# One-core streaming-encoder block: the output projection's mixes transposed one tile ahead, the up projection's products interleaved across groups

## The chip, the cores and the metric

The kernel runs on one core of a Trainium2 chip. The metric is the device time of one execution in microseconds; it was run three times, and one more execution was taken with the hardware profiler. The engines are called PE (matrix products), DVE (vector), ACT (scalar, activation functions), POOL (GpSimd) and SP, whose queue issues all transfers between HBM and the core's memory SBUF. PE writes its results to PSUM, of which the kernel uses eight banks of 512 fp32 columns by 128 rows.

## The reference

One layer of an encoder, all in fp32, over 1024 frames and 16 meta tokens in front of them. Cut to what matters here:

```
n = rms_norm(h); z = n @ w_in
u = silu(layer_norm(causal_conv(a * sigmoid(gate))))          # branch A, 512 columns
o = block_causal_attention(...)                               # branch B, 512 columns
mix = concat(rms_norm(u, conv_out_g), rms_norm(o, attn_out_g))
h = h + mix @ w_out                                           # output projection, 1024 x 1024
n2 = rms_norm(h, ffn_norm_g)
up = causal_depthwise_conv(n2 @ w_ffn_up, ffn_conv_w, ffn_conv_b)   # 1024 -> 2 x 2816, conv of 3 taps
g, val = up[..., :D_FF], up[..., D_FF:]
h = h + (silu(g) * val) @ w_ffn_down                          # 2816 -> 1024
out = rms_norm(h, final_norm_g)                               # meta tokens dropped
```

## The kernel before

Every fp32 product is made of reduced-precision ones. A value is split into a high part (a copy in the type fp32r, made by ACT, L167 for operands and L244 for down weights) and a low part (the difference, made by DVE, L168, or for down weights by POOL, L247), and each product takes three matmuls: high by high, high by low, low by high (`mm3`, L162 to L164). The program is written as one sequence; a scheduler then sets the order of each engine's instructions from the dependences and its own estimate of durations. So an engine's order isn't simply that of the code, but it follows it loosely.

**Output projection.** Tokens come in tiles of 128 rows, in the order 8, 0, 1, ..., 7; tile 8 holds the two meta rows that the later convolution needs. For tile t and branch g (0 is A, 1 is B) `mix_part` transposes the mix by four PE transposes into a bank `mt`, and splits it into `mx`. `project` multiplies it with the split weights: two banks `po`, 12 matmuls of 128x512 each. `add_branch` adds the scaled result to the residual `ht` on DVE (L967). In the loop over tiles, each step transposes the A mix of the tile two steps on, multiplies it at once, transposes the B mix of the tile two steps on, and multiplies the B mix of this tile.

**Norm and spread.** One step behind, `ffn_norm` takes the sum of squares (ACT L978), an inverse root by some ten small DVE instructions (L182 to L193) and the normed tile `n` (DVE L980; also called n2). `spread` transposes `n` into two banks `nt` and makes from it the operands of the up projection. These are kept for a scheme of the Strassen-Winograd kind: seven products in place of eight, on operands B11, B21 (tiles 8, 0 to 3) and B22, T1 to T4 (from tiles 4 to 7, `spread_second`: sums on DVE L861, L862 and POOL L864, L865, then splits). Each has a high and a low part, xB11h, xB11l and so on.

**Up projection.** 22 pairs of column blocks; pair i has 128 gate columns and 128 value columns. `up_weights` makes from two loaded blocks (`raw`) the seven weights A11, S3, S1, S2, A12, A22, S4, with four DVE sums (L888, L891, L894, L901) and seven splits into `uw`. The tokens form two column groups, c = 0 (258 wide) and c = 1 (256 wide). `up_pair` makes the seven products of one pair and group, each 12 matmuls (L920), in four banks `up`: A11·B11, S3·T3, S1·T1, S2·T2, A12·B21, A22·T4, S4·B22. S2·T2 is added in PSUM on top of A11·B11, A22·T4 on top of S3·T3, and S4·B22 on top of S1·T1. Between them ACT copies p1 and u2 out of PSUM (L925, L929), DVE makes u3 (`tmp`, L930) and the four quarters of the two rows (L931, L933, L935, L937). A22·T4 overwrites the bank that u3 is read from, so it can't start before u3 is made. Then `conv3` (ACT L1117, DVE L1118, L1119) for gate and value, the silu (ACT L1149), the product of the two (DVE L1151) and a store to `gated_d`. The weights of pair i+1 are made piece by piece while group c = 1 of pair i is written.

**Down projection.** For each half of the tokens and each of the 22 blocks k: the gated block is loaded from `gated_d` and split (`gate_split`, ACT L1163, DVE L1164), the weight block is split, and 24 matmuls of 128x512 add into eight banks `pd`. After it the final norm is applied and the result stored.

## Time and profile before

| | us |
|---|---|
| runs, lowest, median, highest | 1333.83, 1334.62, 1339.85 |
| the profiled execution | 1330.62 |
| its span, first to last instruction | 1328.8 |
| PE busy | 1211.3 (91%) |
| DVE busy | 901.9 (68%) |
| ACT busy | 544.3 (41%) |
| POOL busy | 332.9 (25%) |

The span of the profiled execution falls into the work ahead of the output projection (to about 455 us), the output projection with norm and spread (to 613), the up projection (to 1068) and the down projection with the final norm. Busy time of PE says only that matmuls were in it, not at which clock; the granted clock of a stretch is given beside it, 1.00 for the higher of its two levels (2.4 GHz) and 0.50 for the lower (1.2 GHz). An idle time in brackets stands ahead of an instruction and names who ended it; a name there is that of the last event seen, and can be a neighbour of the true one.

### The profile page before, as it was taken

How to read it: one execution, taken by the hardware profiler on the slowest of the kernel's cores; microseconds unless marked ns; L12 is line 12 of the kernel's file. 1: busy time of each engine (PE TensorE's matmuls, PEld its weight loads, DVE VectorE, ACT ScalarE, POOL GpSimd, SP SyncE). 2: the span in 40 equal slices, each digit the busy share in tenths (PEclk: the TensorE clock that was granted, in tenths of full speed). 3: DMA queues.
4: the chain of work that ended last, by engine and by line, in shares of the span. 5: the costliest groups of instructions: out<-in, count | busy, mean ns of one | idle time of the engine just before them, and what ended most of it. 6: DMA issues, size and time to landing. Idle time of an engine off the chain costs nothing.

```text
span 1328.8 us, 20317 instructions
## 1 busy us (share of the span) xinstructions
PE 1211.3 (91%) x7867; PEld 1112.6 (84%) x7867; DVE 901.9 (68%) x1600; ACT 544.3 (41%) x1049; POOL 332.9 (25%) x309
## 2 busy tenths in 40 slices
PE   6899598979989888868999999999999979999997
PEld 6799598969877767657999999999999968888886
DVE  6799979848888755487778787787877731233134
ACT  7212344356765622233434443344433343323322
POOL 3244655124556400020000000000000045514540
PEclk9899889989998899897999999999999989999999
DMA  7110110883432121132121212212122245725521
GB/s 254 52 37 13 36 48 31 205 225 92 108 101 80 33 80 64 48 111 96 49 95 65 80 64 80 95 66 80 64 80 94 78 148 194 241 102 183 188 106 64
DMA packets 47397, 130.54 MB, mean 98 GB/s; under 512 B 8282, under 2 KB 12954, under 8 KB 47300
## 3 DMA queue, kind: packets, MB, share of 16 engines
q1 hardware_dynamic: 47300, 129.24, 30.1%
q8 instruction: 62, 1.02, 0.3%
q14 instruction: 35, 0.29, 0.1%
HBM read 98.36 MB, written 28.33 MB: 95 GB/s over the span
## 4 chain that ended last, share of the span: by engine, by line
PE 41%; DVE 12%; ACT 2%; issue 1%; DVEq 0%; ACTq 0%
PE up L920 22%; PE pd L162 6%; PE pd L163 6%; PE pd L164 6%; DVE tg L1118 4%; DVE tg L1119 4%; ACT tg L1117 2%; DVE tg L1151 2%; DVE row L937 1%; DVE tmp L930 1%; DVE t L188 0%; DVE n L980 0%; DVE xT2l L168 0%; PE nt L157 0%; DVE ta L862 0%
## 5 line engine op out<-in xcount | busy, mean ns | idle before, releaser
L247 POOL TENSOR_TENSOR wl<-raw,wh 128x1024 fp32r<-128x1024 f32 (+3 forms) x75 | 196.1, 2620 | 668.6 <-ACT wh L244 645.9
L162 PE MATMUL pd<-wh,gp 128*128 128x512 f32 (+1 forms) x356 | 139.0, 396 | 8.1 <-ACT wh L244 8.1
L163 PE MATMUL pd<-wl,gp 128*128 128x512 f32 (+1 forms) x356 | 139.3, 391 | 0.0
L164 PE MATMUL pd<-wh,gp 128*128 128x512 f32 (+1 forms) x356 | 139.1, 391 | 0.0
L1164 DVE TENSOR_TENSOR gp<-gt,gp 128x512 fp32r<-128x512 f32 x44 | 42.1, 961 | 129.2 <-ACT gp L1163 129.2
L1117 ACT ACTIVATE tg<-row,ffnw 128x1024 f32<-128x1024 f32 x44 | 52.3, 1237 | 126.2 <-DVE row L937 126.2
L681 POOL TENSOR_TENSOR pl<-p,ph 128x320 fp32r<-128x320 f32 (+11 forms) x76 | 79.6, 1052 | 79.5 <-ACT ph L679 48.7
L162 PEld LDWEIGHTS pd<-wh,gp 128*128 128x128 f32 x356 | 68.0, 191 | 23.2 <-ACT wh L244 8.3
L920 PE MATMUL up<-xT4h,uw 128*128 128x258 f32 (+1 forms) x352 | 72.1, 288 | 12.5 <-DVE tmp L930 12.5
L163 PEld LDWEIGHTS pd<-wl,gp 128*128 128x128 f32 x356 | 67.2, 189 | 14.9 <-POOL wl L247 0.2
L164 PEld LDWEIGHTS pd<-wh,gp 128*128 128x128 f32 x356 | 67.2, 189 | 14.9
L920 PE MATMUL up<-xB11h,uw 128*128 128x258 f32 (+1 forms) x352 | 73.3, 286 | 3.9 <-ACT uw L167 2.4
L1118 DVE SCALAR_TENSOR_TENSOR tg<-row,ffnw,tg 128x1024 f32<-128x1024 f32 x44 | 54.6, 1282 | 28.9 <-ACT tg L1117 28.9
L920 PE MATMUL up<-xT3h,uw 128*128 128x258 f32 (+1 forms) x352 | 72.4, 286 | 0.5 <-ACT uw L167 0.5
L920 PE MATMUL up<-xB21h,uw 128*128 128x258 f32 (+1 forms) x352 | 72.5, 281 | 0.0
L673 ACT ACTIVATE p<-st 128x320 f32<-128x320 f32 (+11 forms) x120 | 53.4, 454 | 44.7 <-PE st L671 17.0
L920 PEld LDWEIGHTS up<-xT4h,uw 128*128 128x128 f32 x352 | 57.2, 189 | 16.8 <-DVE tmp L930 16.8
L920 PE MATMUL up<-xT1h,uw 128*128 128x258 f32 (+1 forms) x352 | 70.9, 282 | 0.0
L920 PE MATMUL up<-xB22h,uw 128*128 128x258 f32 (+1 forms) x352 | 70.0, 282 | 0.0
L920 PE MATMUL up<-xT2h,uw 128*128 128x258 f32 (+1 forms) x352 | 70.0, 282 | 0.0
L1163 ACT ACTIVATE gp<-gt 128x512 fp32r<-128x512 f32 x44 | 27.7, 630 | 99.7 <-DMA gt<-gated_d 97.4
L162 PE MATMUL po<-wh,mx 128*128 128x512 f32 x128 | 54.2, 423 | 15.5 <-ACT mx L167 15.5
(286 smaller groups left out, 3765.5 us busy)
## 6 DMA issues: line engine op xcount, KB each, us to landing
raw<-w_up SPq DMA_DIRECT2D x44, 512.0 KB
raw<-w_down SPq DMA_DIRECT2D x44, 512.0 KB
gated_d<-tg SPq DMA_DIRECT2D x22, 512.0 KB
gt<-gated_d SPq DMA_DIRECT2D x44, 256.0 KB
raw<-w_ag SPq DMA_DIRECT2D x8, 512.0 KB
raw<-w_out SPq DMA_DIRECT2D x8, 512.0 KB
ht<-x SPq DMA_DIRECT2D x8, 512.0 KB
h_d<-ht SPq DMA_DIRECT2D x8, 512.0 KB
```

The costliest lines, as they stand in the source:

```text
L162: PE.matmul(ps, lhsT=wh, rhs=xh, start=(first and i == 0), stop=False)
L163: PE.matmul(ps, lhsT=wh, rhs=xl, start=False, stop=False)
L164: PE.matmul(ps, lhsT=wl, rhs=xh, start=False, stop=(last and i == n - 1))
L247: G.tensor_tensor(wl, raw, f(wh), ALU.subtract)
L673: S.activation(p32[:n], ps[:n, :w], AF.Exp, scale=SCALE)
L681: (V if turn[0] % PLV[h] == 0 else G).tensor_tensor(pl[:n], p32[:n], f(ph)[:n], ALU.subtract)
L920: PE.matmul(ps[:, :w], lhsT=wt[:, wj, k], rhs=x[:, k], start=(fresh and k == 0 and wj == 0 and x is xh), stop=(k == 3 and wj == 1), skip_g ...
L1117: S.activation(tg, row[:, 2:2 + SEQ], AF.Identity, scale=ffnw[:, m, 2:3], bias=ffnw[:, m, 3:4])
L1118: V.scalar_tensor_tensor(tg, row[:, 1:1 + SEQ], ffnw[:, m, 1:2], tg, ALU.mult, ALU.add)
L1119: V.scalar_tensor_tensor(tg, row[:, 0:SEQ], ffnw[:, m, 0:1], tg, ALU.mult, ALU.add)
L1163: S.activation(gp[:, 0], src, AF.Copy)
L1164: V.tensor_tensor(gp[:, 1], src, f(gp)[:, 0], ALU.subtract)
```

## The change

The work is the same: the same products, the same splits, the same transfers. What moves is where they are written.

1. **Mixes.** `mix_upto(g, n)` transposes the mixes of branch g up to the n-th tile of the order. In step j the A mix of the tile at place j+4 of the order is transposed, behind the A product of the one at j+2, where before the mix of j+2 was transposed directly ahead of its own product. The B mix is transposed two steps ahead, as before.
2. **First up weights.** The load of pair 0's blocks is issued ahead of the spread of tile 6, and the norm of tile 7 is made, but its spread is written only after the `mid` of the first group.
3. **Groups.** `up_pair` becomes the class `Pairs`, whose products are written in three parts: `head` (A11·B11), `mid` (S3, S1, S2, and `own` = A12·B21) and `tail` (A22·T4, S4·B22). The order is mid of group n, head of group n+1, tail of group n. In pair 0's second group, c = 1 of i = 0, `own` comes first.
4. **Step to the down projection.** After the last group with c = 0 the first down weight is split (`fetch`) and the gated blocks of k = 0 and 1 are loaded and split.

```diff
-        product(b1, "A11", "B11", True)
-        S.activation(p1, b1[:, :w], AF.Copy)
-        product(b3, "S3", "T3", True)
-        product(b4, "S1", "T1", True)
-        product(b1, "S2", "T2", False)
-        S.activation(u2, b1[:, :w], AF.Copy)
-        V.tensor_tensor(u3, b3[:, :w], u2, ALU.add)
...
-        product(b2, "A12", "B21", True)
-        V.tensor_tensor(rows[0][:, first], b2[:, :w], p1, ALU.add)
-        product(b3, "A22", "T4", False)
-        V.tensor_tensor(rows[1][:, first], b3[:, :w], u2, ALU.add)
-        product(b4, "S4", "B22", False)
-        V.tensor_tensor(rows[0][:, second], b4[:, skip:w], u2[:, skip:], ALU.add)
...
+    class Pairs:
...
+        def head(self):
+            w = self.w
+            self.b1, self.b2, self.b3, self.b4 = (bank("up") for _ in range(4))
+            tmp = page("tmp", [P, 3, 258])
+            self.p1, self.u2, self.u3 = (tmp[:, j, :w] for j in range(3))
+            self.product(self.b1, "A11", "B11", True)
+            S.activation(self.p1, self.b1[:, :w], AF.Copy)
+
+        def own(self):
+            self.product(self.b2, "A12", "B21", True)
+            V.tensor_tensor(self.rows[0][:, self.first], self.b2[:, :self.w], self.p1, ALU.add)
+
+        def mid(self):
+            w, skip = self.w, self.skip
+            if self.early:
+                self.own()
+            self.product(self.b3, "S3", "T3", True)
+            self.product(self.b4, "S1", "T1", True)
+            self.product(self.b1, "S2", "T2", False)
+            S.activation(self.u2, self.b1[:, :w], AF.Copy)
+            V.tensor_tensor(self.u3, self.b3[:, :w], self.u2, ALU.add)
+            V.tensor_tensor(self.rows[1][:, self.second], self.b4[:, skip:w], self.u3[:, skip:], ALU.add)
+            if not self.early:
+                self.own()
+
+        def tail(self):
+            w, skip = self.w, self.skip
+            self.product(self.b3, "A22", "T4", False)
+            V.tensor_tensor(self.rows[1][:, self.first], self.b3[:, :w], self.u2, ALU.add)
+            self.product(self.b4, "S4", "B22", False)
+            V.tensor_tensor(self.rows[0][:, self.second], self.b4[:, skip:w], self.u2[:, skip:], ALU.add)
...
+    def mix_upto(g, n):
+        while mixed[g] < min(9, n):
+            mix_part(order[mixed[g]], g)
+            mixed[g] += 1
 
     done_a = 0
+    mix_upto(0, 4)
     for j, t in enumerate(order):
         while done_a < min(9, j + 3):
-            if done_a > 1:
-                mix_part(order[done_a], 0)
             first_branch(order[done_a])
             done_a += 1
-        if j + 2 < 9:
-            mix_part(order[j + 2], 1)
+        mix_upto(0, j + 5)
+        mix_upto(1, j + 3)
         cur = firsts.pop(t)
         add_branch(*cur, project(t, 1), rb)
         prev.append(cur)
         if len(prev) > 1:
+            if j == 8:
+                raws_up[0] = load_up(0), load_up(NFF)
             spread(*ffn_norm(*prev.pop(0)))
-    raws_up[0] = load_up(0), load_up(NFF)
-    while prev:
-        spread(*ffn_norm(*prev.pop(0)))
+    last = ffn_norm(*prev.pop(0))
...
-        up_pair(W, rows, 0, lambda: None)
...
-        up_pair(W, rows, 1, step)
...
+    W = [None] * NFF
+    for w_ in start_pair(0):
+        W[0] = w_
+    made = {}
+    rows_of = {}
+
+    def make(n):
+
+        i, c = divmod(n, 2)
+        if c == 0:
+            rows_of[i] = [page("row", [P, NQ]) for _ in range(2)]
+            made[n] = Pairs(W[i], rows_of[i], c)
+        else:
+            gen = start_pair(i + 1)
+
+            def step():
+                for w_ in gen:
+                    W[i + 1] = w_
+                    break
+
+            made[n] = Pairs(W[i], rows_of[i], c, step, early=(i == 0))
+        made[n].head()
+
+    make(0)
+    for n in range(2 * NFF):
+        made[n].mid()
+        if n == 0:
+            spread(*last)
+        if n + 1 < 2 * NFF:
+            make(n + 1)
+        made.pop(n).tail()
+        if n == 2 * NFF - 2:
+            fetch(at["down", 0, 0] + 1)
+            for s in range(2):
+                gate_split(0, s)
+        i, c = divmod(n, 2)
+        if c == 1:
+            rows = rows_of.pop(i)
+            tg = conv3(i, rows[0])
+            S.activation(tg, tg, AF.Silu)
+            tv = conv3(NFF + i, rows[1])
+            V.tensor_tensor(tg, tg, tv, ALU.mult)
+            SY.dma_start(out=gated_d[i], in_=tg)
...
-    for s in dsteps[:2]:
-        gate_split(*s)
```

How this moves instructions is shown at three places, in rows of the engines' order: line, operation, output<-inputs, shape; "x4" stands for as many in a row. **PE in the output projection.** `mixa` and `mixb` are the mixes of branch A and B, `mt` their transposes, `mx` the split mix, `po` a product. Before:

```order
L157 MATMUL nt_5754<-ident,n_1275_5731 128x2 x4
L157 MATMUL mt_5772<-ident,mixa_3257 128x128 x4
L162 MATMUL po_5781<-wh_4490,mx_5771 128x512
L163 MATMUL po_5781<-wl_4491,mx_5771 128x512
L162 MATMUL po_5782<-wh_4490,mx_5771 128x512
L163 MATMUL po_5782<-wl_4491,mx_5771 128x512
L157 MATMUL mt_5810<-ident,mixb_3222 128x128 x4
L162 MATMUL po_5817<-wh_4813,mx_5623 128x512
L163 MATMUL po_5817<-wl_4814,mx_5623 128x512
```

After, around the transposes of the next A mix:

```order
L162 MATMUL po_5791<-wh_4806,mx_5632 128x512
L163 MATMUL po_5791<-wl_4807,mx_5632 128x512
L164 MATMUL po_5791<-wh_4806,mx_5632 128x512
L157 MATMUL mt_5819<-ident,mixa_3391 128x128 x4
L157 MATMUL mt_5827<-ident,mixb_3222 128x128 x4
L162 MATMUL po_5834<-wh_4813,mx_5640 128x512
L163 MATMUL po_5834<-wl_4814,mx_5640 128x512
L164 MATMUL po_5834<-wh_4813,mx_5640 128x512
```

Before, the first four products read the very mix (mx_5771) that the transposes (mt_5772) right ahead of them give; after, the products on both sides of the transposes read mixes that were transposed at least a tile earlier (mx_5632, mx_5640).

**PE and DVE at the start of the up projection.** `nt` are the transposes of the normed tile `n` (n_1430 is that of the last tile, n_1408 before and n_1410 after that of tile 6). PE before:

```order
L164 MATMUL po_6432<-wh_5129,mx_6251 128x512
L157 MATMUL nt_6478<-ident,n_1408_6460 128x128 x4
L157 MATMUL nt_6483<-ident,n_1408_6460 128x128 x4
L157 MATMUL nt_6537<-ident,n_1430_6519 128x128 x4
L157 MATMUL nt_6542<-ident,n_1430_6519 128x128 x4
L920 MATMUL up_6597<-xB11h_5761,uw_6566 128x258
L920 MATMUL up_6597<-xB11l_5762,uw_6566 128x258
L920 MATMUL up_6599<-xT3h_6334,uw_6570 128x258
```

PE after:

```order
L919 MATMUL up_6570<-xT1h_6327,uw_6548 128x258 x2
L919 MATMUL up_6570<-xT1l_6328,uw_6548 128x258
L919 MATMUL up_6570<-xT1h_6327,uw_6548 128x258
L919 MATMUL up_6568<-xB21h_5783,uw_6555 128x258
L919 MATMUL up_6568<-xB21l_5784,uw_6555 128x258
L157 MATMUL nt_6637<-ident,n_1430_6520 128x128 x4
L919 MATMUL up_6568<-xB21h_5783,uw_6555 128x258
L919 MATMUL up_6567<-xT2h_6331,uw_6552 128x258
```

DVE before, from the last tile's `n` on:

```order
L980 SCALAR_TENSOR_TENSOR n_1430_6519<-ht_6221,r_6521,ffng_5556 128x1024
L861 TENSOR_TENSOR ta_6547<-nt_6537,bf_6092 128x512
L862 TENSOR_TENSOR ta_6547<-nt_6542,ta_6547 128x512
L168 TENSOR_TENSOR xT1l_6499<-ta_6547,xT1h_6498 128x4x128
L888 TENSOR_TENSOR sb_6565<-raw_6514,raw_6516 128x512
L168 TENSOR_TENSOR xB22l_6493<-nt_6542,xB22h_6492 128x4x128
L168 TENSOR_TENSOR xT2l_6503<-ta_6547,xT2h_6502 128x4x128
L891 TENSOR_TENSOR sa_6564<-raw_6516 128x512
L168 TENSOR_TENSOR uw_6566<-raw_6514,uw_6566 128x512
```

DVE after, from the same instruction on:

```order
L996 SCALAR_TENSOR_TENSOR n_1430_6520<-ht_6222,r_6522,ffng_5556 128x1024
L888 TENSOR_TENSOR sb_6539<-raw_6460,raw_6462 128x512
L168 TENSOR_TENSOR uw_6540<-raw_6460,uw_6540 128x512
L891 TENSOR_TENSOR sa_6538<-raw_6462 128x512
L168 TENSOR_TENSOR uw_6544<-sb_6539,uw_6544 128x512
L894 TENSOR_TENSOR sa_6538<-sa_6538,raw_6460 128x512
L168 TENSOR_TENSOR uw_6548<-sa_6538,uw_6548 128x512
L901 TENSOR_TENSOR sb_6539<-raw_6460,sa_6538 128x512
L168 TENSOR_TENSOR uw_6552<-sa_6538,uw_6552 128x512
L168 TENSOR_TENSOR uw_6555<-raw_6460,uw_6555 128x512
L168 TENSOR_TENSOR uw_6558<-raw_6462,uw_6558 128x512
L168 TENSOR_TENSOR uw_6562<-sb_6539,uw_6562 128x512
```

The last tile's transposes stood ahead of all up products and now come after three whole products and two matmuls of a fourth. On DVE the last tile's sums `ta` stood ahead of the first weights' sums and low parts (`sb`, `sa`, `uw`); now all eleven of these stand directly behind `n`, and the last tile's L861 comes three rows further on.

**PE in the last pair.** `up_11645` to `up_11648` before and `up_11619` to `up_11622` after are the banks of its group c = 1. PE before, the end of S2·T2 and the start of A22·T4 of c = 1:

```order
L920 MATMUL up_11645<-xT2h_6502,uw_11481 128x256 x2
L920 MATMUL up_11645<-xT2l_6503,uw_11481 128x256
L920 MATMUL up_11645<-xT2h_6502,uw_11481 128x256
L920 MATMUL up_11647<-xT4h_6510,uw_11515 128x256
L920 MATMUL up_11647<-xT4l_6511,uw_11515 128x256
```

PE after, the start of A22·T4 of c = 0 (`up_11507`):

```order
L919 MATMUL up_11620<-xB21h_6116,uw_11499 128x256 x2
L919 MATMUL up_11620<-xB21l_6117,uw_11499 128x256
L919 MATMUL up_11620<-xB21h_6116,uw_11499 128x256
L919 MATMUL up_11507<-xT4h_6339,uw_11535 128x258
L919 MATMUL up_11507<-xT4l_6340,uw_11535 128x258
L919 MATMUL up_11507<-xT4h_6339,uw_11535 128x258 x2
L919 MATMUL up_11507<-xT4l_6340,uw_11535 128x258
```

PE after, behind the end of S2·T2 of c = 1:

```order
L919 MATMUL up_11619<-xT2h_6507,uw_11481 128x256 x2
L919 MATMUL up_11619<-xT2l_6508,uw_11481 128x256
L919 MATMUL up_11619<-xT2h_6507,uw_11481 128x256
L162 MATMUL pd_11770<-wh_11665,gp_11669 128x512
L163 MATMUL pd_11770<-wl_11666,gp_11669 128x512
L162 MATMUL pd_11771<-wh_11665,gp_11669 128x512
L163 MATMUL pd_11771<-wl_11666,gp_11669 128x512
```

Before, A22·T4 follows S2·T2 of its own group directly (in group c = 0 with six matmuls between). After, the A22·T4 of c = 0 stands behind three products and A12·B21 of the other group, as it does in the pairs before it with 36 to 48 matmuls between; and behind the last S2·T2 come 18 matmuls of the down projection (`pd`) ahead of the last A22·T4.

## Rows read from the trace of the kernel before

**Rows 1.** The page, part 1: busy time, share of the span, instructions.

```profile
PE 1211.3 (91%) x7867; PEld 1112.6 (84%) x7867; DVE 901.9 (68%) x1600; ACT 544.3 (41%) x1049; POOL 332.9 (25%) x309
```

**Rows 2.** Table by stage: stretch, length, busy (instructions) by engine, granted clock, DMA, GB/s.

```profile
466.80:470.00 3.20, 3.14 (x10) 2.63 (x11) 1.99 (x10) 1.51 (x6) 0.00 (x0) 0.53 0.27 68
470.00:542.00 72.00, 60.95 (x296) 49.29 (x294) 39.67 (x99) 18.67 (x38) 0.00 (x0) 1.00 0.22 78
542.00:548.30 6.30, 6.21 (x17) 4.94 (x18) 2.31 (x3) 0.64 (x2) 0.00 (x0) 0.50 0.00 1
...
591.20:613.20 22.00, 8.73 (x37) 7.71 (x37) 20.39 (x37) 11.15 (x20) 5.75 (x4) 0.61 0.36 120
613.20:1068.20 455.00, 442.35 (x3670) 437.86 (x3669) 347.80 (x558) 183.58 (x298) 0.00 (x0) 1.00 0.22 78
1068.20:1081.00 12.80, 4.86 (x12) 3.81 (x13) 7.69 (x9) 8.11 (x10) 4.78 (x2) 0.60 0.24 78
1081.00:1322.00 241.00, 240.93 (x1058) 197.02 (x1056) 66.89 (x109) 78.73 (x121) 103.63 (x43) 1.00 0.46 158
```

**Rows 3.** List of PE's waits, 455 to 613: total us, times, longest.

```profile
PE po L162 <- ACT mx L167: 15.5, 7, 3.7
PE nt L157 <- DVE n L980: 8.9, 1, 8.9
...
PE up L920 <- ACT uw L167: 2.9, 2, 2.4
PE up L920 <- DVE uw L168: 1.4, 1, 1.4
```

**Rows 4.** Timeline of PE: start, length, instruction, [idle before <-what ended it].

```profile
466.86 0.80 PE L162 MATMUL po<-wh,mx 128*128 128x512 f32 x1 [2.58 <-ACT mx L167]
...
480.45 0.50 PE L162 MATMUL po<-wh,mx 128*128 128x512 f32 x1 [1.83 <-ACT mx L167]
...
495.39 0.50 PE L162 MATMUL po<-wh,mx 128*128 128x512 f32 x1 [2.00 <-ACT mx L167]
...
542.10 0.80 PE L162 MATMUL po<-wh,mx 128*128 128x512 f32 x1 [3.66 <-ACT mx L167]
542.69 0.63 PE L163 MATMUL po<-wl,mx 128*128 128x512 f32 x1
543.12 0.63 PE L162 MATMUL po<-wh,mx 128*128 128x512 f32 x1
```

**Rows 5.** Table by stage, the spreads of tiles 4 to 6.

```profile
572.00:582.00 10.00, 6.12 (x30) 4.74 (x28) 9.79 (x25) 5.39 (x12) 3.60 (x4) 1.00 0.29 105
```

**Rows 6.** Timeline of DVE around the last tile's spread.

```profile
598.82 1.28 DVE L980 SCALAR_TENSOR_TENSOR n<-ht,r,ffng 128x1024 f32<-128x1024 f32 x1
...
603.37 1.76 DVE L888 TENSOR_TENSOR sb<-raw,raw 128x512 f32<-128x512 f32 x1
...
609.13 0.68 DVE L894 TENSOR_TENSOR sa<-sa,raw 128x512 f32<-128x512 f32 x1
```

**Rows 7.** Timeline of POOL in the same stretch.

```profile
603.00 1.58 POOL L864 TENSOR_TENSOR tb<-ta,bf 128x512 f32<-128x512 f32 x1 [7.05 <-DVE ta L862]
```

**Rows 8.** List of PE's waits, 613 to 1068.

```profile
PE up L920 <- DVE tmp L930: 12.5, 21, 1.5
```

**Rows 9.** Timeline of DVE, end of one pair in the up loop.

```profile
886.55 2.48 DVE L1118 SCALAR_TENSOR_TENSOR tg<-row,ffnw,tg 128x1024 f32<-128x1024 f32 x2 [1.31 <-ACT tg L1117]
888.95 2.47 DVE L1119 SCALAR_TENSOR_TENSOR tg<-row,ffnw,tg 128x1024 f32<-128x1024 f32 x2
891.52 1.23 DVE L1151 TENSOR_TENSOR tg<-tg,tg 128x1024 f32<-128x1024 f32 x1
```

**Rows 10.** Timeline of PE, the first down matmul.

```profile
1076.14 1.22 PE L162 MATMUL pd<-wh,gp 128*128 128x512 f32 x2 [8.05 <-ACT wh L244]
```

**Rows 11.** Timeline of ACT after the last up product.

```profile
1068.59 2.37 ACT L1117 ACTIVATE tg<-row,ffnw 128x1024 f32<-128x1024 f32 x2 [4.10 <-DVE row L937]
...
1075.05 2.94 ACT L244 ACTIVATE wh<-raw 128x1024 fp32r<-128x1024 f32 x3
```

More of the change, by code (lines that the diff above doesn't have):

```diff
@@ L903, in up_weights @@
         yield W
-    def up_pair(W, rows, c, step):
-        w = SCH[c][1] - SCH[c][0]
-        o1 = SCH[c][0]
-        skip = 2 if c == 0 else 0
-        o2 = HALF + (0 if c == 0 else 256)
-        first, second = slice(o1, o1 + w), slice(o2, o2 + 256)
-        b1, b2, b3, b4 = (bank("up") for _ in range(4))
-        tmp = page("tmp", [P, 3, 258])
-        p1, u2, u3 = (tmp[:, j, :w] for j in range(3))
-        def product(ps, wn, xn, fresh):
-            (xh, xl), wt = xs[c, xn], W[wn]
-            for k in range(4):
-                for wj, x in ((0, xh), (0, xl), (1, xh)):
-                    PE.matmul(ps[:, :w], lhsT=wt[:, wj, k], rhs=x[:, k], start=(fresh and k == 0 and wj == 0 and x is xh),
-                              stop=(k == 3 and wj == 1), skip_group_check=True)
-            step()
-        product(b1, "A11", "B11", True)
-        S.activation(p1, b1[:, :w], AF.Copy)
-        product(b3, "S3", "T3", True)
-        product(b4, "S1", "T1", True)
-        product(b1, "S2", "T2", False)
-        S.activation(u2, b1[:, :w], AF.Copy)
-        V.tensor_tensor(u3, b3[:, :w], u2, ALU.add)
-        V.tensor_tensor(rows[1][:, second], b4[:, skip:w], u3[:, skip:], ALU.add)
-        product(b2, "A12", "B21", True)
-        V.tensor_tensor(rows[0][:, first], b2[:, :w], p1, ALU.add)
-        product(b3, "A22", "T4", False)
-        V.tensor_tensor(rows[1][:, first], b3[:, :w], u2, ALU.add)
-        product(b4, "S4", "B22", False)
-        V.tensor_tensor(rows[0][:, second], b4[:, skip:w], u2[:, skip:], ALU.add)
@@ new lines, in block_kernel, with __init__, product @@
+    class Pairs:
+        def __init__(self, W, rows, c, step=lambda: None, early=False):
+            self.W, self.rows, self.c, self.step, self.early = W, rows, c, step, early
+            self.w = SCH[c][1] - SCH[c][0]
+            o1, o2 = SCH[c][0], HALF + (0 if c == 0 else 256)
+            self.first, self.second = slice(o1, o1 + self.w), slice(o2, o2 + 256)
+            self.skip = 2 if c == 0 else 0
+        def product(self, ps, wn, xn, fresh):
+            (xh, xl), wt = xs[self.c, xn], self.W[wn]
+            for k in range(4):
+                for j, (wj, x) in enumerate(((0, xh), (0, xl), (1, xh))):
+                    PE.matmul(ps[:, :self.w], lhsT=wt[:, wj, k], rhs=x[:, k], start=(fresh and k + j == 0),
+                              stop=(k == 3 and j == 2), skip_group_check=True)
+            self.step()
+        def head(self):
[26 more added lines that the diff above has]
+            V.tensor_tensor(self.rows[0][:, self.second], self.b4[:, skip:w], self.u2[:, skip:], ALU.add)
@@ L1120, in conv3 @@
         return tg
-    gated_d = dram.tile([NFF, P, SEQ], F32, name="gated_d")
-    def start_pair(i):
-        if i < NFF and i not in raws_up:
-            raws_up[i] = load_up(i), load_up(NFF + i)
-        return up_weights(i, raws_up.pop(i)) if i < NFF else iter(())
-    W = None
-    for W in start_pair(0):
-        pass
-    for i in range(NFF):
-        ahead = start_pair(i + 1)
-        rows = [page("row", [P, NQ]) for _ in range(2)]
-        up_pair(W, rows, 0, lambda: None)
-        nxt = []
-        def step():
-            for w_ in ahead:
-                nxt.append(w_)
-                break
-        up_pair(W, rows, 1, step)
-        for w_ in ahead:
-            nxt.append(w_)
-        if nxt:
-            W = nxt[-1]
-        tg = conv3(i, rows[0])
-        S.activation(tg, tg, AF.Silu)
-        tv = conv3(NFF + i, rows[1])
-        V.tensor_tensor(tg, tg, tv, ALU.mult)
-        SY.dma_start(out=gated_d[i], in_=tg)
-    fg = page("fg", [P, D])
-    SY.dma_start(out=fg, in_=a["final_norm_g"].partition_broadcast(P))
     gps = {}
@@ L1165, in gate_split @@
         gps[half, k] = gp
+    W = [None] * NFF
[36 more added lines that the diff above has]
+            SY.dma_start(out=gated_d[i], in_=tg)
+    fg = page("fg", [P, D])
+    SY.dma_start(out=fg, in_=a["final_norm_g"].partition_broadcast(P))
     dsteps = [(half, k) for half in range(2) for k in range(NFF)]
-    for s in dsteps[:2]:
-        gate_split(*s)
     def down(ps, half, t, c0, c1, k0, k1, first, last):
```

6 lines of the change are left out of this document (added).

## The prediction

> **What bounds the kernel now.** I began with the busy shares: PE is at work for 1211.3 of 1328.8 us, DVE for 902, no other engine for more than 545 [rows 1]. So a change that leaves PE's matmuls as they are can only win the time in which PE waits, or in which it runs at the lower of its two clock levels. The table by stage says where that time is [rows 2]: the output projection (455 to 591.2), the step into the up projection (591.2 to 613.2: PE busy 8.73 of 22.0 us), the up loop (613.2 to 1068.2: 442.35 of 455.0) and the step into the down projection (1068.2 to 1081.0: 4.86 of 12.8). From 1081 to 1322 PE is busy for 240.93 of 241.0 us at full clock and nothing can be won. The list of PE's waits names who ended them: ACT's `mx` in the projection (15.5 us in 7 waits), DVE's `n` before the up projection (8.9) and ACT's and DVE's `uw` behind it (2.9 and 1.4) [rows 3], DVE's `tmp` in the loop (12.5 in 21) [rows 8], and ACT's `wh` at the end (8.05) [rows 10]. The change touches all four places. The matmuls number two more than before; I price nothing for them.
>
> **Part A, mixes one tile ahead.** Before, the four transposes of a tile's branch A stand directly ahead of the 24 matmuls that read them, and PE waits for ACT's high part and then DVE's low part; 1.8 to 2.0 us per tile [rows 4]. Now the 24 matmuls behind a transpose read a mix that was transposed at least a tile earlier, so ACT and DVE have 24 x 0.23 = 5.5 us (240.93 us for 1058 instructions in the steady down stage, [rows 2]) for what took them under 2. The first wait (2.58) has only four more transposes put ahead of it; between 0 and 2.58 I let it keep 1.2; the other six (12.95) go, so do 1.4 of the first: 14.3. Two waits also cost clock: after the 2.58 the next 3.2 us have a granted clock of 0.53, after the 3.66 the next 6.3 us have 0.50 [rows 2], and the spacing there is 0.43 instead of 0.23 us a matmul [rows 4]. After waits of 1.8 to 2.0 us the clock stays at 1.00 [rows 2]. Lost: 3.2 x 0.47 + 6.3 x 0.50 = 4.6; I count 4.1, as some of it is transposes. **A = -18.4.** What is late next is DVE: 39.67 us of work in 72.0 there [rows 2], 55%; at 12.9 us a tile (14.94, the distance of two waits [rows 4], less the second's 2.0) that is 64%. It becomes tight only from tile 4's spread on, where DVE is busy 98% of the time [rows 5].
>
> **Part B, the first group ahead of the last tile's spread.** DVE works all but without a gap [rows 5] through the spreads of tiles 4 to 6 and makes the last tile's `n` at 598.82 [rows 6]; PE waits 8.9 us for it, transposes, then waits 2.9 and 1.4 for the first weights' splits, of which DVE's part stands behind pieces of the last spread [rows 3, 6]. By 613.2 PE has done 28 up matmuls, at a mean clock of 0.61 [rows 2]. The change puts the weights' eleven DVE instructions behind `n` and ahead of the spread, and three products ahead of the last tile's transposes. The 8.9 itself stays: the splits still follow `n` on DVE. And `n` of tile 6 now stands behind three more instructions of tile 5's spread and a residual add (0.7 to 1.4 us more for tile 6, some 0.7 for tile 7). In the old time scale: `n` ends at 600.1 + 0.7 = 600.8, `sb` and the first low part take 2 x 0.6, so PE starts at 602.0; some 4 us at the lower clock (0.215 us a matmul, half the rate of the loop's 0.1206, which is 442.35 over 3670) are 19 matmuls; the other 6.2 us to 612.2 hold eight transposes and about 41 more. So 60 matmuls stand at 612.2 against 28 at 613.2: 1.0 + 32 x 0.1206 = **-4.9**. Bounds: if half of the splits come late as before, 0; if `n` isn't later (0.7), the clock is back 2 us sooner (9 matmuls at 0.1) and the first split comes two DVE instructions sooner (1.2), -8. One price in it hangs on a row: `sb` took 1.76 us beside POOL's L864, and 0.68 is what its like took with POOL idle (L894) [rows 6, 7]. I take 0.6 to 0.68, as POOL's work on the last tile now comes later. The Trainium skill ("SBUF — State Buffer", section "Who interferes with whom") says that a DVE instruction with two SBUF inputs and a GpSimd one that reads SBUF hold one read port in turn and the second waits in full. The row at 603.37 agrees in direction (1.1 us longer); by that rule alone the same delay would only move to the last tile's splits, and B stays.
>
> **Part C, products interleaved.** In each pair T4's product waits for `u3`, which stands on DVE behind the gate multiply of the pair before: L1151 runs from 891.52 for 1.23, `u3` comes right behind it, then T4; 21 waits, 12.5 us, 0.6 each [rows 8, 9]. The clock is 1.00 all through the loop [rows 2], so a wait costs its length and no more. Now 36 to 48 matmuls of the other group (4.3 to 5.8 us) stand between T2 and T4, so a `u3` that is 0.6 late isn't seen. **C = -12.5.** What is late next: DVE has 347.8 of 455.0 us (16 a pair) and its block of conv and multiply is 886.55 to 892.75, 6.2 us in one piece [rows 9]. Behind it now stand the next pair's first low parts as well. Following the rows of the new order with these durations, the tightest split is ready about 0.5 us before PE wants it, others 2 us and more; nothing shown can be gained beyond 12.5, and the bound on the other side is a part of the waits staying, 0 at worst unless the block shifts (below). The Trainium skill ("TensorE: Matmul & The Clock Gate", section "A second HAM failure mode: psum-queue depth-cycling") says that frequent short idles between groups of matmuls make the clock swing between its levels. The loop has 21 such idles at a granted clock of 1.00; the row decides, and no clock is given back here. By the page C would have been larger by whatever part ran at the lower level.
>
> **Part D, the first down weights early.** PE's last up product ends at 1068.1 (1076.14 less 8.05); ACT then has two L1117, a gate part, the silu, a gate part and only at 1075.05 the first `wh`, so PE stands for 8.05 us [rows 10, 11] and restarts at the lower clock: 12 matmuls in 4.86 us [rows 2], 0.405 each instead of 0.23, 2.1 lost. That is 10.2. Now the first weight's split and two gate splits come before the last group's end, and 18 of the first 24 down matmuls (18 x 0.23 = 4.1 us) stand ahead of the last T4. The second weight's `wh` is still behind both L1117 on ACT: these start 0.5 us after the last matmul and take 2.37, `wh` 1.0, so it is ready at +3.9, while PE has 6 matmuls, 1.4 us. It waits 2.6, about what cost the clock at 466.86 [rows 2, 4], so 2.1 more: 4.7 in place of 10.2, **D = -5.5**, from -3 (the early weight arrives late and PE waits ahead of T4) to -9 (no wait long enough to lower the clock).
>
> **Sum.** -18.4 - 4.9 - 12.5 - 5.5 = -41.3. The profiled execution took 1330.62 us (span 1328.8), the median of the runs is 1334.62, 4.0 more. Against the profile 1289.3; against the median **1293**.
>
> **Rivals.**
> (1) *DVE takes part of A back.* From 572 on it has no slack [rows 5]. If the stretch with spreads is DVE's and not PE's from the first of them, the last two tiles' 1.86 each aren't won, and B's gain, which rests on DVE too, goes: +3.7 + 4.9, **1302**. For: 98% busy; against: the stretch begins after the seven waits, so it starts earlier as a whole.
> (2) *The loop's wait only moves.* The gap of 0.6 returns at another instruction, a low part of the next weights behind the gate multiply: C = 0, **1305**. For: 0.5 us of slack by my count. Against: PE runs a product or more ahead of it.
> (3) *Slower: DVE's block meets two open groups.* A group's four banks are freed by DVE's sums, and with heads issued early two groups hold all eight. If the sums of one group slip behind the 6.2 us block, the next head's products wait for a bank as well as for splits. It decides at 41.3 / 21 = 1.97 us per pair; a sum that waits out the whole 6.2 us with only 36 matmuls (4.3 us) of cover costs 1.9 us, 21 x 1.9 = 40, 1333; with the length of the waiting sum itself (some 0.4) it is 2.3, 21 x 2.3 = 48, and the time **1341**. For: the block is one piece. Against: in the new order sums stand between its parts, and DVE is at 76% in the loop.
> (4) *The step to the down projection gives nothing*, because the early weight holds PE ahead of T4: **1299**.
> (5) *It doesn't do what it says.* The scheduler already mixes groups (before, six matmuls of the other group stand between the first group's T2 and its T4), so the new order could be the old one. The rows of the order speak against it; no change, about 1334.
>
> **How the numbers follow.** Forecast 1293: 0.57. (1) 0.13, (2) 0.13, (4) 0.08, two of these together (1310 to 1316) 0.03. (3) 0.04, (5) 0.02. The forecast's own bounds are B -8 and D -9 below (1286.4), and a few us of each term above. The range 1282 to 1313 leaves out the slower cases, (5) and the tails. A difference of 0.5%, 6.7 us, is about what a measurement of this kernel can tell from none. All cases up to 1316 are faster by more: 0.94; (5) and a mild form of (3) are the same, 0.03; slower 0.03.
>
> **What would show it.** A: no wait of PE for `mx` but the first, clock 1.00 from 470 on, tiles some 13 us apart. B: up matmuls ahead of the last `nt`, one wait of 8 to 11 us left before them. C: no wait for `tmp`, 20.26 us a pair. D: a wait of 2 to 3 us for `wh` in place of 8.05, 18 `pd` matmuls ahead of the last T4. It is wrong if PE's list shows waits for `uw` or for DVE's sums in every pair, or if `nt` waits for `n` earlier than at tile 5.

## The result and the profile after

The changed kernel took 1288.49 us (median of four runs, 1286.58 to 1290.09), the kernel before 1335.22 beside it (1333.83 to 1339.85). The ratio is 0.9644 with a 95% interval of 0.9617 to 0.9671: 47 us less. The forecast was 1293, the range 1282 to 1313. The profiled execution has a span of 1288.3 us against 1328.8.

| | before | after |
|---|---|---|
| span | 1328.8 | 1288.3 |
| PE busy | 1211.3 | 1201.9 |
| DVE busy | 901.9 | 906.0 |
| ACT busy | 544.3 | 542.7 |
| POOL busy | 332.9 | 335.7 |

The table by stage of the changed kernel answers to [rows 2]; columns are stretch, length, busy (instructions) of PE, weight loads, DVE, ACT and POOL, granted clock, share and GB/s of the transfers:

```profile
470.00:565.00 95.00, 91.35 (x447) 75.00 (x445) 64.31 (x159) 30.24 (x63) 3.37 (x4) 1.00 0.25 89
565.00:590.00 25.00, 14.33 (x66) 12.29 (x67) 23.52 (x52) 12.49 (x23) 6.09 (x5) 0.73 0.25 86
...
600.00:1026.00 426.00, 426.00 (x3569) 426.00 (x3568) 342.82 (x552) 182.01 (x297) 3.40 (x2) 1.00 0.22 80
1026.00:1050.00 24.00, 18.47 (x91) 14.70 (x91) 15.51 (x12) 7.71 (x9) 8.93 (x3) 0.99 0.27 96
1050.00:1060.00 10.00, 9.83 (x36) 7.46 (x36) 1.40 (x2) 3.17 (x4) 3.97 (x2) 0.84 0.65 205
```

From 600 to 1026 PE never idles, at full clock. The list of PE's waits from 440 on (total us, times, longest) answers to [rows 3, 8, 10]:

```profile
PE nt L157 <- DVE n L996: 6.0, 2, 4.0
PE up L919 <- ACT uw L167: 5.0, 1, 5.0
PE up L919 <- DVE uw L168: 3.4, 1, 3.4
PE pd L164 <- DVE gp L1158: 2.6, 1, 2.6
PE pd L162 <- ACT wh L244: 2.4, 1, 2.4
PE po L162 <- ACT mx L167: 0.9, 1, 0.9
PE pd L163 <- POOL wl L247: 0.6, 1, 0.6
PE pd L162 <- ACT gp L1157: 0.2, 1, 0.2
```

The seven waits for `mx` are one of 0.9, the 21 for `tmp` are gone, and the one of 8.05 for `wh` is 2.4. New is the wait for `gp`. Of the two for `n` the one of 4.0, at tile 5, stood before as well (3.98 ahead of 582.10, listed under DVE's `v` and so not in [rows 3]). The 8.9 ahead of the last tile, with the 2.9 and 1.4 for the first weights behind it, is now 2.01 at tile 6 and then 4.96 and 3.37 for those weights: 10.3 in place of 13.2.

**Where the time went.** Four transposes late in the attention (`ot`) start at 432.25 before and at 435.71 after: ahead of all changed work this execution is 3.5 us later, 2.3 of it within the first 30 us, so 3.46 is taken off each difference. Four marks then cut the rest: the transposes of tile 5's `n` (582.10 and 565.33), the 100th up matmul (621.79 and 599.68), the end of the last one (1068.09 and 1033.55, with 18 down matmuls, 4.1 us, done ahead of it after), and the 1000th down matmul (1308.52 and 1268.01).

| part | forecast | by the traces |
|---|---|---|
| A, to tile 5's transposes | -18.4 | -16.77 - 3.46 = -20.2 |
| B, to the 100th up matmul | -4.9 | -22.11 - 3.46 + 20.23 = -5.3 |
| C, to the last up matmul | -12.5 | -12.43 - 4.10 = -16.5 |
| D, to the 1000th down matmul | -5.5 | -5.97 + 4.10 = -1.9 |
| sum | -41.3 | -44.0 |

The sum was nearly right because two errors cancel, which is luck: C gave 4.0 us more than forecast, D 3.6 less. The medians differ by 46.7, 2.7 more than the parts explain; the interval of the ratio reaches 3.6 us to either side. The experiments take the parts one by one; a difference of two ratios is turned into us with 1335, since the kernel before took 1335.4 to 1337.3 us beside these runs, and each ratio's own interval reaches 2 to 4 us to either side.

### The profile page after: what moved, and what is told of

Same layout as the page of the kernel before. It is cut to its first block, busy times and chain, and to the rows that moved or that the text cites. A ratio compares the mean times of both kernels' runs of the same rounds, so it can differ in the third digit from the quotient of the medians.

```text
span 1288.3 us, 20332 instructions
## 1 busy us (share of the span) xinstructions
PE 1201.9 (93%) x7867; PEld 1108.6 (86%) x7867; DVE 906.0 (70%) x1600; ACT 542.7 (42%) x1049; POOL 335.7 (26%) x309
## 4 chain that ended last, share of the span: by engine, by line
PE 65%; DVE 5%; DMA 1%; ACT 1%; issue 1%; DVEq 0%; SPq 0%; POOL 0%; ACTq 0%; POOLq 0%
PE up L919 34%; PE pd L162 6%; PE pd L163 6%; PE pd L164 6%; PE po L162 2%; PE po L164 2%; PE po L163 2%; DVE pl L681 1%; PE acc L702 1%; PE acc L704 1%; PE acc L703 1%; PE st L669 1%; PE st L670 1%; PE nt L157 1%; PE st L671 1%
## 5 line engine op out<-in xcount | busy, mean ns | idle before, releaser
L163 PEld LDWEIGHTS pd<-wl,gp 128*128 128x128 f32 x356 | 67.3, 189 | 15.7 <-POOL wl L247 1.0
L1147 DVE SCALAR_TENSOR_TENSOR tg<-row,ffnw,tg 128x1024 f32<-128x1024 f32 x44 | 54.6, 1282 | 29.5 <-ACT tg L1146 29.5
L244 ACT ACTIVATE wh<-raw 128x1024 fp32r<-128x1024 f32 (+2 forms) x66 | 65.8, 1006 | 4.7 <-DMA raw<-w_uqn 4.1
L646 DVE TENSOR_REDUCE mp<-smax 128x1 f32<-128x264 f32 (+9 forms) x120 | 53.8, 476 | 19.9 <-PE smax L645 19.2
```

The source lines that it names most:

```text
L163: PE.matmul(ps, lhsT=wh, rhs=xl, start=False, stop=False)
L244: S.activation(wh, raw, AF.Copy)
L646: anchor[0] = V.tensor_reduce(mp[:n, 3 * j + pc:3 * j + pc + 1], ps[:n, :k1 - k0], AX.X, ALU.max).ins
L1147: V.scalar_tensor_tensor(tg, row[:, 1:1 + SEQ], ffnw[:, m, 1:2], tg, ALU.mult, ALU.add)
```

## The experiments

**A undone.** The mixes are transposed at their use again.

```diff
-    mix_upto(0, 4)
...
         while done_a < min(9, j + 3):
+            mix_upto(0, done_a + 1)
             first_branch(order[done_a])
             done_a += 1
-        mix_upto(0, j + 5)
         mix_upto(1, j + 3)
```

> The changed kernel with part A alone undone: the A mixes are transposed directly ahead of their own product, as before. By the comparison of the two traces part A is worth 20.2 us (15.5 of listed waits, 4.6 of lower clock): 1308 to 1309 us against 1288.5. If only the waits count and the clock would have recovered anyway: 1304. If DVE takes part A back in the stretch with the spreads (the first rival), undoing it costs less: 1300 to 1305. Waits of PE for mx: six or seven, one over 2.5 us with a granted clock of about 0.5 behind it.

Measured 1312.71 us, ratio 0.9815 (0.9797 to 0.9833): 0.0171 or 23 us slower than the changed kernel. PE waits for `mx` seven times, 15.5 us, as before, and the clock falls behind the two long ones. The table by stage of this kernel:

```profile
469.00:473.00 4.00, 3.55 (x12) 2.93 (x13) 2.38 (x10) 2.31 (x6) 0.00 (x0) 0.59 0.31 91
544.00:551.00 7.00, 6.37 (x17) 5.09 (x18) 2.78 (x5) 1.18 (x3) 0.00 (x0) 0.51 0.05 20
```

In its trace tile 5's transposes come at 584.59, 20.1 us later when the `ot` mark is taken off; by the 1000th down matmul 0.9 more has come, and the rest of the 23 is within the interval. The first rival falls: nothing of A is taken back by DVE.

**The spread first.** The last tile's spread stands ahead of the first weights and products.

```diff
+    spread(*last)
     W = [None] * NFF
...
-        if n == 0:
-            spread(*last)
```

> The changed kernel with the first half of part B undone: the last tile's spread is written ahead of the first weights and products. By the traces part B is worth 5.5 us: 1294. If PE's start is set by DVE's queue whatever stands first in it, the order of the two is worth nothing: 1288 to 1290. The last tile's transposes stand ahead of all up products, and between them PE waits 2 to 5 us for uw.

Measured 1292.71, ratio 0.9678 (0.9659 to 0.9697): 4.5 us slower; the two intervals overlap a little. The 100th up matmul comes 5.5 us later. The order is worth about what the traces gave for part B. The edit isn't quite alone in its effect: the scheduler now puts 9 and not 18 down matmuls ahead of the last up matmul, and by the 1000th down matmul the run is 3.5 us behind. The earlier load of the first weights, the other half of the change there, wasn't undone in any run.

**C undone.** Each group is written whole, the next pair's first product behind the conv.

```diff
         made[n].mid()
-        if n + 1 < 2 * NFF:
-            make(n + 1)
         made.pop(n).tail()
...
             SY.dma_start(out=gated_d[i], in_=tg)
+        if n + 1 < 2 * NFF:
+            make(n + 1)
```

> The changed kernel with part C undone: each group is written whole, and the next pair's first product is written behind the conv and the gate multiply. In its order five matmuls of the other group stand between T2 and T4 in every first group, as before. Theory: a wait costs its listed idle time of 0.6 us and 0.27 more, because the last matmul ahead of it drains (0.28 instead of 0.12 us) and the first behind it starts slowly (0.22): about 20 waits, 1304 to 1306. Rival: a wait costs what is listed: 1300 to 1301. Granted clock 1.00 all through the loop.

Measured 1305.18, ratio 0.9762 (0.9745 to 0.9780): 15.8 us slower. Its list of PE's waits from 600 to 1030:

```profile
PE up L919 <- DVE tmp L943: 9.9, 19, 0.8
```

So 9.9 us of listed waiting (10.4 with a twentieth wait behind 1030) cost 15.8 us. The timeline of PE in the kernel before shows how (start, length, instruction, idle before it):

```profile
892.20 0.28 PE L920 MATMUL up<-xB21l,uw 128*128 128x256 f32 x1
892.32 0.28 PE L920 MATMUL up<-xB21h,uw 128*128 128x256 f32 x1
893.14 0.39 PE L920 MATMUL up<-xT4h,uw 128*128 128x258 f32 x1 [0.54 <-DVE tmp L930]
893.37 0.28 PE L920 MATMUL up<-xT4l,uw 128*128 128x258 f32 x1
893.48 0.41 PE L920 MATMUL up<-xT4h,uw 128*128 128x258 f32 x2
```

In a stream matmuls start every 0.12 us although each lasts 0.28. The listed idle time begins when the last one has ended, 0.28 after its start, and behind the wait the second matmul starts 0.23 after the first. The matmul at 893.14 starts 0.82 after the one before it, not 0.12: 0.70 lost, and 0.11 more behind it, 0.81 for 0.54 listed. Over the 21 waits of the kernel before, the starts around a wait lie 0.877 and 0.224 apart in the mean against 0.119 in the stream: 21 x 0.86 = 18.1 us for 12.5 listed. The same sum over the 20 waits of the run with C undone gives 15.7, and 15.8 was measured. The stream itself is 0.0004 us a matmul slower in the changed kernel, 1.6 us in some 3590, which makes 16.5 and meets the 16.5.

**Groups in turn, head ahead of the conv.** The cutting is undone, but the next pair's first product stays where the change put it, ahead of the conv.

```diff
-        if n + 1 < 2 * NFF:
-            make(n + 1)
         made.pop(n).tail()
+        if n + 1 < 2 * NFF:
+            make(n + 1)
```

> The changed kernel with each group written whole (its last two products ahead of the next group's first), but the next pair's first product still ahead of the conv and the gate multiply. In its order 24 to 60 matmuls stand between T2 and T4, nearly as in the changed kernel. Theory: what makes part C is that the next pair's first product is written ahead of the conv, and the cutting of a group into three parts is not needed: 1287 to 1290, no wait for tmp. Rival: the cut itself counts, some of the 21 waits of 0.6 come back: 1295 and more.

Measured 1288.87, ratio 0.9650 (0.9630 to 0.9670), the same as the changed kernel, with no wait for `tmp`. The three parts of a group aren't what counts: the scheduler interleaves on its own once the next pair's first product is written ahead of the conv.

**D undone.** First down weight and gate splits behind the loop.

```diff
-        if n == 2 * NFF - 2:
-            fetch(at["down", 0, 0] + 1)
-            for s in range(2):
-                gate_split(0, s)
...
+    for s in range(2):
+        gate_split(0, s)
```

> The changed kernel with part D undone: the first down weight and the first two gate splits are written behind the loop. By the traces part D is worth 1.9 us, not the forecast's 5.5: 1290.4 by the traces, 1294 by the forecast. One wait of 8 us for wh, restart at the lower clock, and DVE's L1148 at 2.5 us for two (not 6.8), since POOL starts on wl only when the conv is done.

Measured 1290.57, ratio 0.9654 (0.9637 to 0.9670): 1.3 us slower, which can't be told from none; its trace gives 2.1 for the part up to the 1000th down matmul. Here the rows that explain it are those of DVE and POOL. Timeline of the kernel with D undone, DVE and POOL:

```profile
1033.57 2.47 DVE L1148 SCALAR_TENSOR_TENSOR tg<-row,ffnw,tg 128x1024 f32<-128x1024 f32 x2
...
1036.56 1.22 DVE L1198 TENSOR_TENSOR tg<-tg,tg 128x1024 f32<-128x1024 f32 x1
...
1037.53 10.60 POOL L247 TENSOR_TENSOR wl<-raw,wh 128x1024 fp32r<-128x1024 f32 x4 [438.57 <-ACT wh L244]
```

Timeline of the changed kernel, DVE, POOL and then PE:

```profile
1037.72 6.77 DVE L1148 SCALAR_TENSOR_TENSOR tg<-row,ffnw,tg 128x1024 f32<-128x1024 f32 x2
1044.60 3.22 DVE L1202 TENSOR_TENSOR tg<-tg,tg 128x1024 f32<-128x1024 f32 x1
1047.74 0.68 DVE L1158 TENSOR_TENSOR gp<-gt,gp 128x512 fp32r<-128x512 f32 x1
...
1037.45 5.96 POOL L247 TENSOR_TENSOR wl<-raw,wh 128x1024 fp32r<-128x1024 f32 x2 [12.68 <-ACT wh L244]
1043.77 2.96 POOL L247 TENSOR_TENSOR wl<-raw,wh 128x1024 fp32r<-128x1024 f32 x1 [0.36 <-ACT wh L244]
...
1048.47 0.50 PE L164 MATMUL pd<-wh,gp 128*128 128x512 f32 x1 [2.58 <-DVE gp L1158]
```

With D undone POOL makes its low parts when DVE's conv is over. With D they run beside it: the two L1148 take 6.77 us for 2.47, the multiply 3.22 for 1.22, and the gate split of k = 2, queued on DVE behind both, is late. PE waits 2.58 us for it and runs at a clock of 0.84 from 1050 to 1060. The late multiply also holds up SP's queue, where its store stands ahead of the load of the next gated block. SP's wait in the changed kernel, from its list:

```profile
SPq L1203 <- DVE tg L1202: 7.4, 1, 7.4
```

In the run with groups in turn the same wait of 2.58 left the clock at 1.00, and PE then waited 1.20 us for that next block, 0.17 in the changed kernel: without the lower clock the late block takes its place.

**POOL beside the conv, on purpose.** Work for POOL whose results nobody uses, in six pairs of the loop.

```diff
             rows = rows_of.pop(i)
+            if i in (6, 7, 8, 12, 13, 14):
+                d1 = page("pr", [P, D])
+                G.tensor_tensor(d1[:, :8], rows[0][:, 1016:1024], rows[0][:, 1016:1024], ALU.subtract)
+                for _ in range(3):
+                    if i < 12:
+                        G.tensor_tensor(d1, rows[0][:, :D], rows[0][:, :D], ALU.subtract)
+                    else:
+                        G.memset(d1, 0.0)
             tg = conv3(i, rows[0])
```

> The changed kernel with POOL work added beside DVE's conv in six pairs of the up loop, whose results nobody uses: in pairs 6 to 8 three subtractions of 128x1024 that read SBUF, in pairs 12 to 14 three fills of the same size that only write it. Theory (POOL instructions that read SBUF hold up DVE instructions with two SBUF inputs): L1147, L1148 and L1202 of pairs 6 to 8 take 2 to 3 times their 1.28 and 1.2 us, as at the end of the loop in the changed kernel (6.77 for two), PE waits some us in these pairs, and pairs 12 to 14 are as without. Rival (DVE was slowed at the end by the transfers or by ACT): both kinds leave DVE's lengths as they are.

Measured 1298.48 in a single run. Timeline of DVE in pair 6, beside three subtractions of POOL, and of POOL there:

```profile
731.64 4.94 DVE L1147 SCALAR_TENSOR_TENSOR tg<-row,ffnw,tg 128x1024 f32<-128x1024 f32 x2 [1.37 <-ACT tg L1146]
736.50 2.91 DVE L1148 SCALAR_TENSOR_TENSOR tg<-row,ffnw,tg 128x1024 f32<-128x1024 f32 x1
739.67 1.27 DVE L1148 SCALAR_TENSOR_TENSOR tg<-row,ffnw,tg 128x1024 f32<-128x1024 f32 x1
...
730.77 7.56 POOL L1204 TENSOR_TENSOR pr<-row 128x1024 f32<-128x1024 f32 x3
```

The same in pair 12, beside three fills:

```profile
863.32 2.48 DVE L1147 SCALAR_TENSOR_TENSOR tg<-row,ffnw,tg 128x1024 f32<-128x1024 f32 x2 [1.37 <-ACT tg L1146]
865.72 1.28 DVE L1148 SCALAR_TENSOR_TENSOR tg<-row,ffnw,tg 128x1024 f32<-128x1024 f32 x1
...
862.44 2.98 POOL L1206 MEMSET pr<- 128x1024 f32 x3
```

As long as POOL subtracts, DVE's instructions take about twice as long, 4.94 us for two and 2.91 for one; when POOL is done at 738.33 the second L1148 is back at 1.27; beside fills nothing changes. The first L1148 starts at 736.50 and ends at 739.41, 1.08 after POOL's last: it waited that one out and then took nearly its own length. The contention is shown, and that it hangs on POOL reading SBUF. The Trainium skill ("SBUF — State Buffer", section "Who interferes with whom") states just this: a DVE instruction with two SBUF inputs contends with a GpSimd one that reads SBUF and not with one that only writes. The prediction named the rule for part B, where it moved nothing, and didn't put it to part D, where it decides.

**Two low parts on DVE.** POOL is kept out of DVE's conv; its next low parts start at 1040.85, when the conv is done.

```diff
-            G.tensor_tensor(wl, raw, f(wh), ALU.subtract)
+            (V if key in (("down", 0, 1), ("down", 0, 2)) else G).tensor_tensor(wl, raw, f(wh), ALU.subtract)
```

> The changed kernel with the low parts of the down weights k = 1 and 2 made by DVE and not by POOL, so that POOL is idle while DVE makes the last conv. Theory of the contention: the two L1148 take 2.5 us and not 6.8, L1202 1.2 and not 3.2; DVE takes 2.4 us more for the two low parts; the waits of PE for gp (2.58) and wl (0.57) and the lower clock behind them (2 to 2.5) go: 1283 to 1285 against 1288.5. Rival (part D is bounded by ACT's order, wh behind the conv): the 2.38 us for wh is all that matters, and the time stays within 1 us, or rises by 2.4 for DVE's extra work.

Measured 1283.59, ratio 0.9605 (0.9583 to 0.9627): 5.2 us faster than the changed kernel (the two intervals overlap a little; from the last up matmul to the 1000th down matmul the trace gives 4.7). Timeline of DVE:

```profile
1036.92 1.28 DVE L1148 SCALAR_TENSOR_TENSOR tg<-row,ffnw,tg 128x1024 f32<-128x1024 f32 x1
1038.12 1.22 DVE L247 TENSOR_TENSOR wl<-raw,wh 128x1024 fp32r<-128x1024 f32 x1
1039.26 1.28 DVE L1148 SCALAR_TENSOR_TENSOR tg<-row,ffnw,tg 128x1024 f32<-128x1024 f32 x1
...
1042.19 1.22 DVE L1202 TENSOR_TENSOR tg<-tg,tg 128x1024 f32<-128x1024 f32 x1
```

DVE does more work and is done some 4 us sooner; no wait for `gp` is left (2.4 for `wh` and 0.7 for `wl` are) and the clock is 1.00 from 1050 on.

**Three down weights early.** The other way round the stretch.

```diff
-            fetch(at["down", 0, 0] + 1)
-            for s in range(2):
+            fetch(at["down", 0, 0] + 3)
+            for s in range(3):
...
-            if s + 2 < len(dsteps):
-                gate_split(*dsteps[s + 2])
+            if s + 3 < len(dsteps):
+                gate_split(*dsteps[s + 3])
```

> The changed kernel with three down weights and three gate splits, not one and two, written ahead of the last group's end. By the sum of the waits at the end (2.38 + 0.57 + 2.58 and about 2.5 of lower clock) up to 8 us can go: 1281 to 1283. Against it: in its order the copy u2 of the last group stands on ACT behind three copies of 128x1024 (1.0 us each) and T4 comes directly behind T2, so PE should wait 3 to 4 us for tmp there: 1284 to 1286. POOL's three low parts fall into the last two products, where DVE has no conv, and L1148 stays at 2.5 us for two.

Measured 1280.94, ratio 0.9589 (0.9568 to 0.9610): 7.3 us faster than the changed kernel, the fastest of all. Its two L1148 take 4.63 us beside POOL and not the 2.5 that were expected, but PE has the 72 down matmuls of three weights to run meanwhile and waits for nothing; the wait that I feared ahead of T4 is 0.93, not 3 to 4.

**Two weights a pair earlier**, with the low parts of k = 2 and 3 on DVE.

```diff
+        if n == 2 * NFF - 4:
+            fetch(at["down", 0, 0] + 2)
         if n == 2 * NFF - 2:
-            fetch(at["down", 0, 0] + 1)
```

> The kernel with two low parts on DVE (there 1283.6), with two down weights written a pair earlier, so that PE has 24 more matmuls, 5.5 us, beside the last conv, and the low parts of k = 2 and 3 on DVE. Theory: the wait of 2.4 us for wh and the one of 0.7 for wl go, with the lower clock behind them if there is any: 1279 to 1281. Against it: POOL's two low parts now fall beside the conv of the last pair but one, and by the contention seen with added POOL work DVE's L1147 there take up to twice as long, so that PE may wait about 2 us for tmp in that pair: 1282 to 1284.

Measured 1285.64, ratio 0.9625 (0.9606 to 0.9644), some 2.7 us slower than with one weight (the intervals overlap). The time lies above both expected ranges. The waits for `wh` and `wl` are gone as expected, though one of 1.60 for `gp` is new, and POOL's two low parts (from 1002.63, 5.98 us) now fall beside DVE's sums for the last pair's weights. Timeline of DVE, then PE:

```profile
1004.17 2.21 DVE L888 TENSOR_TENSOR sb<-raw,raw 128x512 f32<-128x512 f32 x1
...
1006.65 2.52 DVE L891 TENSOR_TENSOR sa<-raw 128x512 f32<-128x512 f32 x1
...
1009.82 0.51 PE L919 MATMUL up<-xT3h,uw 128*128 128x258 f32 x2 [2.21 <-DVE uw L168]
```

DVE's sums, not the conv, are what is stretched here; the mechanism is the one seen above.

**The first group earlier still.** It is written ahead of the spread of tile 6 too.

```diff
-            if j == 8:
+            if j == 7:
                 raws_up[0] = load_up(0), load_up(NFF)
-            spread(*ffn_norm(*prev.pop(0)))
+            six = ffn_norm(*prev.pop(0))
+            if j < 8:
+                spread(*six)
     last = ffn_norm(*prev.pop(0))
...
         if n == 0:
-            spread(*last)
+            spread(*six)
         if n + 1 < 2 * NFF:
             make(n + 1)
         made.pop(n).tail()
+        if n == 0:
+            spread(*last)
```

> The changed kernel with the first up weights and the first group written ahead of the spread of tile 6 as well, whose operands that group doesn't read, and their blocks loaded one tile earlier. PE's waits before the up loop in the changed kernel are 3.98 + 2.01 + 4.96 + 3.37 with a clock of 0.81 and 0.56 around them. Theory (PE waits there for DVE's queue and for nothing else): DVE's work is the same, but PE has 84 matmuls, 10 us, to do beside the last two spreads: the waits of 2.01, 4.96 and 3.37 shrink to one of about 3 to 4 and the clock comes back sooner, 1280 to 1283. Rival: the loads or the free buffers for the first blocks come too late, or the second group's operands are then late by as much: 1287 to 1290.

Measured 1285.85, ratio 0.9629 (0.9606 to 0.9652), 2 us faster than the changed kernel, which can't be told from none and lies between the two expected ranges; by the marks in the trace the loop ends 0.7 us sooner. The theory fell, and what the rival named, late operands of the second group, is there. The 100th up matmul comes some 9 us sooner, and all but that is lost behind it. Timeline of PE:

```profile
586.35 1.09 PE L157 MATMUL nt<-ident,n 128*128 128x128 f32 x8 [1.69 <-DVE n L996]
...
593.35 0.58 PE L919 MATMUL up<-xT2h,uw 128*128 128x256 f32 x1 [4.49 <-ACT xT2h L167]
...
595.03 0.58 PE L919 MATMUL up<-xT2l,uw 128*128 128x256 f32 x1 [1.10 <-DVE xT2l L168]
```

The second group waits for the last tile's operands instead. Between 562 and 600 DVE is busy for 36.59 of 38 us, so its total work is what seems to set when this stretch ends, whatever PE's order within it; no run made that work smaller, so this is argued and not shown.

**Both edits.** The earlier group and two low parts on DVE together.

> Both edits, the first group ahead of the spread of tile 6 and the two low parts on DVE. They touch different stages, so the gains should add: 1275 to 1279. If one of them only shifts a wait that the other meets again, less than the sum of the two.

Measured 1283.65, ratio 0.9607 (0.9585 to 0.9629), the same as with the low parts alone. The expected sum of two gains isn't there. By the marks the loop ends 0.8 us sooner than with the low parts alone, as the run above would have it, and the step to the down projection takes the same: its wait of 0.7 for `wl` is gone, but the clock fell after the 2.39 for `wh`.

## Why the prediction was right, and where it wasn't

**What bounds the kernel** held: with PE's matmuls unchanged the time fell by PE's waits and by its time at the lower clock.

**Part A** was right in every step, and a little small. Of the 2.58 us wait 0.91 stayed, where 1.2 was assumed, and the lower clock cost the 4.6 us that the rows gave, not the 4.1 that I counted; that makes 19.2 of the 20.2. The last 1.0 is 0.2 us for each of the six waits that went. What part C shows, that a wait costs more than its listed idle time, would give as much; here it wasn't worked out matmul by matmul.

**Part B** came to 5.3 for 4.9, the time nearly right and the way there less so. Tile 6's `n` was 2.6 us later in relation to tile 5's, not 0.7 to 1.4: two low parts and a residual add ahead of it took 1.9, and DVE stood idle for 0.9 around tile 5's transposes. The last `n` was 1.0 later, forecast 0.7. Of the one wait of 8 to 11 us that was to be left, three stand there, 2.01, 4.96 and 3.37, together 10.3. The spread-first run confirms the order's share, and the earlier-group run points at its limit, DVE.

**Part C** had the right mechanism and an undersized term: the step "a wait costs its length and no more" failed. It is true of the clock, which stayed at 1.00, but each listed 0.6 us cost 0.86 in starts of matmuls, 18.1 for 12.5. Of the things feared behind it none came: PE's list shows no wait for `uw` or for a sum in the loop, so the second and third rival fall. The rule of the Trainium skill ("TensorE: Matmul & The Clock Gate", section "A second HAM failure mode: psum-queue depth-cycling"), which I had set against the row, gave nothing here: with the short idles gone the granted clock in the loop is 1.00 as it was.

**Part D** is the step that failed, by its size and below its own bounds of 3 to 9: 1.9. The early weight was in time (18 down matmuls run unbroken ahead of T4 from 1026.43), and the wait for `wh` is 2.38 for the 2.6 that was forecast. What was left out is a wait that takes its place: `gp` of k = 2, behind a conv that POOL's low parts stretch from 2.47 to 6.77 us. Behind its 2.58 us the clock was 0.84 over 10 us, while it stayed at 1.00 behind the 2.38. The sum had followed ACT's queue alone, and no sentence asked what is queued on DVE, or what POOL runs beside. The fourth rival, no gain, came nearer in size, but for the wrong reason: the early weight didn't hold PE ahead of T4.

**The fifth rival**, that the change doesn't do what it says, holds a piece of truth: its cutting of the groups does nothing by itself, and the loop's order comes from where the next pair's first product is written.

## What to carry to other kernels

A short wait in a stream of pipelined matmuls costs its listed idle time and the drain and restart around it: here 0.86 us for 0.6. When work is brought forward, ask on every engine what it will now run beside, not only what it is queued behind: low parts on POOL next to a DVE conv ate most of part D. Where one engine is busy nearly all through a stretch, as DVE is between tile 5 and the loop, a new order on the others may only move the wait, as the earlier first group did.
